# A hybrid decoder layer: GLA values and output gates by seven products of halves, placed among another branch's units

## The chip, the cores and the metric

The kernel runs on one core of one Trainium2 chip. The metric is the device time of one execution in microseconds (us). On the core, TensorE (PE) multiplies matrices, VectorE (DVE) and ScalarE (ACT) do elementwise work, GpSimd (POOL) and SyncE (SP) issue transfers. Each engine runs its own list of instructions in order and waits for the others by semaphores; a matmul writes to one of eight PSUM banks, and a bank is reused only when its reader has read it.

## The reference

One layer on 512 tokens of width 1024, all in float32. Cut to what matters:

```python
h = rms_norm(x, norm_mix)
z_rnn, z_q, z_k, z_v, z_g, z_dec, z_mq, z_gate = split(h @ w_in)       # v, g: 768 wide, dec: 16
out_a = rg_lru(causal_dwconv(z_rnn))                                   # branch 0, a linear recurrence
alpha = log_sigmoid(z_dec @ w_decay + b) / 16
o = rms_norm_per_head(chunked_gla(z_q, z_k, z_v, alpha))               # branch 1, 4 heads: dk 96, dv 192
out_b = o * silu(z_g)
out_c = cross_attention(z_mq, mem)                                     # branch 2
merged = sum over branches of sigmoid(z_gate[n]) * (out[n] @ w_branch[n])
x = x + merged @ w_out
x = x + (gelu(gate) * val) @ w_down,   gate, val = causal_dwconv(rms_norm(x) @ w_up)
return rms_norm(x)
```

In chunked_gla, q is scaled by exp(g), k by exp(-g) and by exp(g_last - g), where g is the running sum of alpha in a chunk.

## The kernel before

A float32 product is made of three products at a faster matmul type: each operand is split into a high and a low half (`split`: ACT copies the high half, DVE subtracts it to get the low one), and `mm3` adds high x high, high x low and low x high in one PSUM bank. So a product of 512 tokens with 1024 inputs and n outputs takes 4 token tiles x 8 slices x 3 = 96 matmuls with n moving columns.

The program is a list of **units** and **steps**. A unit is a weight tile with the product that uses it: SP loads the tile ('raw', three buffers), ACT and DVE split it into 'whi' and 'wlo' (three buffers each), and this is issued two units ahead (`AHEAD`). Steps are other work; `weave(units, steps)` spreads steps evenly behind units. A scheduler at build time orders each engine's instructions out of this list. Intermediates live in slots of 512 columns: `fslot` for float32 (named f in the profile), `rslot` for split halves (r), `mslot` (m). Five PSUM banks (mm) serve the large products, three (sm) the small ones.

For each of the three branches and eight column blocks d, `branch(n, acts, d)` gives two units: the gate (24 matmuls of 512 columns from hh and hl, the halves of h; ACT takes its sigmoid, L541, which frees the bank) and the projection of the branch's output (18 matmuls of 512 columns; DVE multiplies it by the gate, L547 or L549, and adds it, L550). The order is branch 2, then 0, then 1. Around the change the program runs:
- branch 2's sixteen units (b2), woven with the recurrence of branch 0: squares, scans (L630), gates, and the split of its output into r tiles by `split`;
- `v_units(0)`: the first half of v with the decay inputs beside it (400 columns), 96 matmuls, copied out by ACT (L682);
- branch 0's sixteen units (b0), woven with the decay steps: `decay_in`, four `decay_logit`, `decay_log`, four `decay_apply` (exponentials on ACT, the products with q and k on DVE, L748 to L753);
- v_units(1) and g_units(0) (384 columns), woven with `k_end` (transposes of the scaled k, L760), `intra` (scores) and `state`;
- g_units(1) and eight held gates for branch 1 (`hold`), woven with `gla_out` (the output of one token tile and two heads, and its norm, per tile) and `gla_flip` (the transpose back to channels);
- branch 1's projections, w_out, and the second half of the layer.

In that second half `down_fast` already does a product of w_down by seven products of halves in place of eight: operands are quartered, sums of quarters are multiplied, and the results are combined. The sums of weight quarters are made by DMAs that add into the tile in SBUF (`accum_op`, on POOL's queue).

Of the kernel before, what the change touches and what calls it, by code (L numbers as in the profile page):

```python
# [8 lines left out]
F32 = mybir.dt.float32  # L9
# [9 lines left out]
P = 128  # L19
# [21 lines left out]
NRAW = 3  # L41
# [14 lines left out]
def trunk(ctx: ExitStack, tc: tile.TileContext, x, xT, mem, memT, par, wdecay, wch, wvd, wvg, wmk,  # L56
# [221 lines left out]

    hh = hpool.tile([P, KD, S], F32R, name="hh", tag="hh")
# [182 lines left out]

    def piece(ps, i):
# [179 lines left out]

    each = lambda fn, bs: [lambda b=b: fn(b) for b in bs]
# [10 lines left out]
    weave(b2[12:], each(lru_square, hi) + [lambda: lru_root(1)] + each(lru_scan, hi))  # L655
# [52 lines left out]
    ea, gc = [], []  # L708

# [83 lines left out]
    def gla_out(t, hp):  # L793
        ps = sbank((P, 2, DV))
        for j in range(2):
            h = 2 * hp + j
            nc.tensor.matmul(ps[:, j, :], lhsT=sT[h][:, t, :], rhs=vt[t][hp][:, j, :], start=True, stop=t == 0)  # L797
            if t:
                nc.tensor.matmul(ps[:, j, :], lhsT=qi[h][:, t * P:(t + 1) * P], rhs=states[hp][t][:, j, :],  # L799
                                 start=False, stop=True)  # L800
        o = fslot((P, 2, DV))
        nc.vector.tensor_copy(o, ps)
        ss, tot = stat(2), stat(2)
        for j in range(2):
            meansq(o[:, j, :], ss[:, j:j + 1], DV)
        nc.vector.tensor_scalar(out=tot, in0=ss, scalar1=EPS, scalar2=None, op0=ALU.add)
        y = rsqrt(tot)
        for j in range(2):
            g = sg[t][hp][:, j, :]
            nc.vector.scalar_tensor_tensor(out=g, in0=o[:, j, :], scalar=y[:, j:j + 1], in1=g,  # L810
                                           op0=ALU.mult, op1=ALU.mult)
# [46 lines left out]
    def gain_rows(src):  # L858
        gb[0] = hpool.tile([P, D], F32, name=nm("gain"), tag="gain")
        with tc.issue_after(loads[-1].ins):  # L860
            nc.sync.dma_start(gb[0], src)
# [98 lines left out]

    HT = S // 2
    kept = {}

    def down_fast(at, np, acts, first, last):


        raw, w, a_in, a_sp, banks = {}, {}, {}, {}, {}

        def src(q, p):
            return wdown[at + p, int(q[1]) - 1, int(q[2]) - 1]

        def load(q, p):
            raw[q, p] = [fslot() for _ in range(2)]
            for j in range(2):
                loads.append(nc.sync.dma_start(raw[q, p][j], src(q, p)[:, j, :]))  # L980

        def add(to, q, p):

            for j in range(2):
                nc.gpsimd.dma_start(raw[to, p][j], src(q, p)[:, j, :], accum_op=ALU.add)  # L985

        def ready(key, q, p):
            hi = wpool.tile([P, 2, S], F32R, tag="whi", name=nm("whi"))
            lo = wpool.tile([P, 2, S], F32R, tag="wlo", name=nm("wlo"))
            if q in ("B21", "B22"):  # L990
                t = wpool.tile([P, 2, S], F32, tag="raw", name=nm("raw"), bufs=NRAW)
                loads.append(nc.sync.dma_start(t, src(q, p)))
                split(hi, lo, t)
            else:
                for j in range(2):
                    split(hi[:, j, :], lo[:, j, :], raw[q, p][j])
            w[key, p] = hi, lo
# [54 lines left out]
        def run(key, p):  # L1052
            (hi, lo), ws = a_sp.pop((key, p)), w.pop((key, p))
            b = key[0]
            for i in range(2):
                if key[1] == "1" and p == 0:
                    banks[b, i] = bank()
                tk = slice(i * P, (i + 1) * P)
                mm3(banks[b, i], [(hi[:, j, tk], lo[:, j, tk], ws[0][:, j, :], ws[1][:, j, :]) for j in range(2)],
                    key[1] == "1" and p == 0, p == np - 1, key[1] != "1")  # L1060
                if p == np - 1:
                    read(key, i, banks[b, i])

        pre = {
            "a1": ("B11", [(6, lambda p: load("B11", p)), (3, sums)]),
            "a2": ("B21", []),
            "c1": ("B11", [(6, lambda p: add("B11", "B12", p))]),
            "c2": ("B22", [(3, sum4)]),
            "b1": ("B11", [(6, lambda p: add("B11", "B22", p))]),
            "b2": ("B12", [(10, lambda p: load("B12", p)), (7, lambda p: add("B12", "B22", p))]),  # L1070
            "b3": ("B11", [(6, lambda p: add("B11", "B21", p))]),
        }
        us = []
        for key, (q, before) in pre.items():
            for p in range(np):
                us.append(([(n, lambda f=f, p=p: f(p)) for n, f in before] +
                           [(AHEAD, lambda key=key, q=q, p=p: ready(key, q, p)),
                            (1 if key == "a1" else 2, lambda key=key, p=p: act_ready(key, p))],
                           lambda key=key, p=p: run(key, p)))
        return us  # L1080

    def final_left(t):

        b = stat(1)
        nc.vector.tensor_scalar(out=b, in0=msq[t][:, 0:1], scalar1=EPS, scalar2=None, op0=ALU.add)
        xg = fslot()
        nc.gpsimd.tensor_tensor(out=xg, in0=x2[t][0], in1=gb[0][:, :HB], op=ALU.mult)
        lefts[t] = b, xg
# [3 lines left out]
    def final(t):  # L1092
# [6 lines left out]
        nc.vector.tensor_tensor(out=xr, in0=x2[t][1], in1=gb[0][:, HB:], op=ALU.mult)  # L1099
# [18 lines left out]
    for fast, up in ((down_fast(0, 3, acts[0], True, False), up_units(range(12, 20), acts[1].append)),  # L1118
                     (down_fast(3, 2, acts[1], False, True), up_units(range(20, NF), halves))):
        for i, u in enumerate(up):  # L1120
            unit(*u)
            for f in fast[len(fast) * i // len(up):len(fast) * (i + 1) // len(up)]:
                made_unit(*f)
# [7 lines left out]
def _layouts(np, v):  # L1131
# [45 lines left out]
    for j in range(3):  # L1177
# [9 lines left out]
        "wch": wch, "wvd": tok(np.concatenate([vv[:, :384], dec], axis=1), 400),  # L1187
        "wvg": np.concatenate([tok(vv[:, 384:], 384), tok(gg, 384)]),
# [26 lines left out]
```

## Time and profile before

| what | value |
|---|---|
| median of 3 runs | 940.05 us (939.97 to 940.52) |
| profiled execution, own time | 940.39 us |
| its span (first to last instruction) | 938.7 us |
| granted TensorE clock, mean | 0.998 |
| busy: PE, DVE, ACT, POOL | 927.6, 612.0, 483.1, 47.4 us |
| end of branch 2's last product | 258.09 us from the span's start |
| v_units(0) | 258.09 to 275.58 us |
| transfers | 106.46 MB, 113 GB/s on average |

In the rows below the columns of a timeline are: start, duration, engine, source line, operation, output <- inputs by name, shape, count, and in brackets the idle time before with its releaser. Durations of matmuls overlap, so the time of one is read from the starts of neighbours.

### The profile page before, as it was taken

To read this page: it belongs to the slowest core of one execution; us is meant where nothing else is said; L and a number is where in the kernel's file an instruction comes from. 1 tells how busy PE (TensorE), PEld (TensorE's weight loads), DVE (VectorE), ACT (ScalarE), POOL (GpSimd) and SP (SyncE) were. 2 spreads that over 40 slices of the span, in tenths; PEclk is the share of its full clock that TensorE was granted. 3 is DMA by queue.
4 is the path that set the end of the run, shared out by engine and by line. 5 is a ranking of instruction groups with operands and counts; after the bars stand their busy time and mean duration, and the time that the engine had idled before them with its cause. 6 is when DMAs were issued, how large, how long until landed. Compare 5 with 4: busy or idle time off the path is not lost.

```text
span 938.7 us, 11903 instructions
## 1 busy us (share of the span) xinstructions
PE 927.6 (99%) x4462; PEld 787.4 (84%) x4462; DVE 612.0 (65%) x1113; ACT 483.1 (51%) x767; POOL 47.4 (5%) x67
## 2 busy tenths in 40 slices
PE   8999999999999999999999999999999999999996
PEld 7899888888897789998888898888888888888885
DVE  7897745565754584475566665555686676598765
ACT  7655545685875765333334424344355444445544
POOL 0000000000000000000000000000010130012102
PEclk9999999999999999999999999999999999999999
DMA  6445212223232223222246401333463685357712
GB/s 230 159 126 189 90 56 72 73 68 99 75 111 96 68 84 102 73 91 84 68 139 224 159 23 45 97 106 112 136 118 134 151 222 124 105 133 180 181 45 90
DMA packets 38043, 106.46 MB, mean 113 GB/s; under 512 B 4369, under 2 KB 5537, under 8 KB 37985
## 3 DMA queue, kind: packets, MB, share of 16 engines
q1 hardware_dynamic: 31648, 94.16, 30.9%
q0 software_dynamic: 5760, 10.49, 6.9%
q10 hardware_dynamic: 576, 1.05, 0.3%
q8 instruction: 35, 0.57, 0.3%
q14 instruction: 24, 0.19, 0.1%
HBM read 103.58 MB, written 2.10 MB: 113 GB/s over the span
## 4 chain that ended last, share of the span: by engine, by line
PE 95%; DVE 3%; ACT 1%; DMA 1%; issue 0%; SPq 0%; ACTq 0%; DVEq 0%
PE mm L102 88%; PE sm L102 3%; PE mm L338 1%; DVE wlo L96 1%; PE sm L797 1%; DMA m<-in_xT 1%; DVE r L96 0%; PE sm L799 0%; PE sm L783 0%; DVE m L306 0%; PE sm L770 0%; PE sm L905 0%; PE sm L818 0%; DVE hl L96 0%; PE sm L512 0%
## 5 line engine op out<-in xcount | busy, mean ns | idle before, releaser
L96 DVE TENSOR_TENSOR wlo<-raw,whi 128x1024 fp32r<-128x1024 f32 (+3 forms) x163 | 179.4, 1104 | 173.8 <-ACT whi L95 79.8
L95 ACT ACTIVATE whi<-raw 128x1024 fp32r<-128x1024 f32 (+3 forms) x163 | 156.5, 964 | 201.1 <-PE mm L102 173.2
L102 PE MATMUL mm<-h2l,whi 128*128 128x512 f32 x360 | 140.1, 389 | 0.0
L102 PE MATMUL mm<-h2h,whi 128*128 128x512 f32 x360 | 139.9, 389 | 0.0
L102 PE MATMUL mm<-whi,r 128*128 128x512 f32 (+1 forms) x440 | 136.8, 381 | 0.0
L102 PE MATMUL mm<-hh,whi 128*128 128x512 f32 x288 | 113.9, 396 | 0.0
L102 PE MATMUL mm<-hl,whi 128*128 128x512 f32 x288 | 112.6, 391 | 0.0
L102 PE MATMUL mm<-r,whi 128*128 128x512 f32 (+1 forms) x448 | 98.3, 368 | 0.0
L102 PEld LDWEIGHTS mm<-whi,r 128*128 128x128 f32 x440 | 82.2, 188 | 14.8
L102 PEld LDWEIGHTS mm<-r,whi 128*128 128x128 f32 x448 | 77.9, 189 | 14.6 <-issue 0.8
L102 PE MATMUL mm<-h2h,wlo 128*128 128x512 f32 x360 | 88.9, 389 | 0.0
L102 PE MATMUL mm<-wlo,r 128*128 128x512 f32 (+1 forms) x220 | 84.0, 382 | 0.2 <-DVE wlo L96 0.2
L102 PEld LDWEIGHTS mm<-h2l,whi 128*128 128x128 f32 x360 | 67.6, 188 | 14.0
L102 PEld LDWEIGHTS mm<-h2h,wlo 128*128 128x128 f32 x360 | 67.6, 188 | 14.1
L102 PEld LDWEIGHTS mm<-h2h,whi 128*128 128x128 f32 x360 | 67.5, 188 | 13.9
L922 DVE SCALAR_TENSOR_TENSOR f<-mm,prm,f 128x511 f32<-128x511 f32 x96 | 71.4, 745 | 6.9 <-ACT f L920 6.1
L102 PE MATMUL mm<-hh,wlo 128*128 128x512 f32 x288 | 71.2, 389 | 0.0
L102 PEld LDWEIGHTS mm<-hh,whi 128*128 128x128 f32 x288 | 54.2, 188 | 11.6 <-issue 0.4
L102 PEld LDWEIGHTS mm<-hh,wlo 128*128 128x128 f32 x288 | 54.1, 188 | 11.2
L102 PEld LDWEIGHTS mm<-hl,whi 128*128 128x128 f32 x288 | 54.1, 188 | 10.7
L985 POOL DMA_DIRECT2D f<-in_wdown x40 | 35.1, 997 | 495.7 <-DMA f<-in_wdown 333.3
L920 ACT ACTIVATE f<-mm,prm 128x512 f32<-128x512 f32 x48 | 37.5, 780 | 35.8 <-PE mm L102 35.8
(212 smaller groups left out, 1340.7 us busy)
## 6 DMA issues: line engine op xcount, KB each, us to landing
raw<-in_wup SPq DMA_DIRECT2D x48, 512.0 KB, 3.5
raw<-in_wch SPq DMA_DIRECT2D x40, 512.0 KB, 3.3
f<-in_wdown POOLq DMA_DIRECT2D x40, 256.0 KB, 5.3
raw<-in_wbr SPq DMA_DIRECT2D x24, 384.0 KB, 3.0
raw<-in_wdown SPq DMA_DIRECT2D x14, 512.0 KB, 3.9
f<-in_wdown SPq DMA_DIRECT2D x20, 256.0 KB, 4.4
raw<-in_wvg SPq DMA_DIRECT2D x12, 384.0 KB, 3.0
raw<-in_wout SPq DMA_DIRECT2D x8, 512.0 KB, 3.6
```

The source lines that it names most:

```text
L95: nc.scalar.activation(hi, src, AF.Copy)
L96: (eng or nc.vector).tensor_tensor(out=lo, in0=src, in1=hi.bitcast(F32), op=ALU.subtract)
L102: nc.tensor.matmul(ps, lhsT=l, rhs=r, start=first and i == 0, stop=last and i == len(seq) - 1, skip_group_check=more)
L338: nc.tensor.matmul(ps[u], lhsT=a, rhs=b, start=q == 0 and i in (0, 2), stop=q == KD - 2 and i >= len(seq) - 2)
L797: nc.tensor.matmul(ps[:, j, :], lhsT=sT[h][:, t, :], rhs=vt[t][hp][:, j, :], start=True, stop=t == 0)
L920: nc.scalar.activation(a, ps, AF.Identity, scale=col(C_FCW + 96 + f), bias=col(C_FCB + f))
L922: nc.vector.scalar_tensor_tensor(out=a[:, j:], in0=ps[:, :S - j], scalar=col(C_FCW + 48 * (2 - j) + f), in1=a[:, j:], op0=ALU.mult, op1=AL ...
L985: nc.gpsimd.dma_start(raw[to, p][j], src(q, p)[:, j, :], accum_op=ALU.add)
```

## The change

**Seven products.** The units of v (with the decay inputs, padded to 2 x 400 columns) and of g are replaced by `seven`, a general form of `down_fast`'s code: h is quartered into token halves and input halves, the weights into input halves and output halves. The seven products are called a1, a2, c1, c2, b1, b2, b3; each has two units (p = 0, 1) of 12 matmuls, of 400 columns for v and 384 for g. a1 and a2 share two banks, c1 and c2 two, and so on: a product whose name ends in 2 or 3 adds onto the bank after the first has been read. B11 is loaded into slots six units ahead; B12, B22 and B21 are added to it in place, by POOL's queue.

**Sums of h.** c1, c2, b1 and b2 need sums of quarters of h. `h_sums` makes them in two steps woven in at the end of branch 2's last four units: four adds hh + hl, four combinations and four splits for each p, 24 instructions on DVE and 8 on ACT.

**Order.** `blend` puts the 28 new units behind the first seven units of branch 0, four behind each. The decay steps go over the rest of branch 0 and two held gates (eleven units); the other GLA steps follow held gates two to seven.

**q and k** are written to DRAM by POOL when they are made, and read back by `qk_back` at the start of the decay steps. **The norm** of the GLA outputs is taken for four token tiles at once (`gla_norm`). There are four raw buffers in place of three, and the gain rows lie in two slots.

```diff
+    def seven(src, n, np, lhs, pre, read, far=AHEAD):
...
+        def add(to, q, p):
+            for j in range(2):
+                nc.gpsimd.dma_start(raw[to, p][j], src(q, p)[:, j, :], accum_op=ALU.add)
...
+        def run(key, p):
+            ws = w.pop((key, p))
+            b = key[0]
+            for i in range(2):
+                if key[1] == "1" and p == 0:
+                    banks[b, i] = bank((P, n))
+                mm3(banks[b, i], [(*lhs(key, p, j, i), ws[0][:, j, :], ws[1][:, j, :]) for j in range(2)],
+                    key[1] == "1" and p == 0, p == np - 1, key[1] != "1")
+                if p == np - 1:
+                    read(key, i, banks[b, i])
+        steps = {
+            "a1": ("B11", [(6, lambda p: load("B11", p))]),
+            "a2": ("B21", [(far, lambda p: direct("B21", p))]),
+            "c1": ("B11", [(6, lambda p: add("B11", "B12", p))]),
+            "c2": ("B22", [(far, lambda p: direct("B22", p))]),
+            "b1": ("B11", [(6, lambda p: add("B11", "B22", p))]),
+            "b2": ("B12", [(10, lambda p: load("B12", p)), (7, lambda p: add("B12", "B22", p))]),
+            "b3": ("B11", [(6, lambda p: add("B11", "B21", p))]),
+        }
...
+    def blend(us, fast, steps=()):
+        for i, u in enumerate(us):
+            unit(*u)
+            for l, f in ((fast, lambda v: made_unit(*v)), (steps, step)):
+                for v in l[len(l) * i // len(us):len(l) * (i + 1) // len(us)]:
+                    f(v)
...
     def qk_evac(ps, i):
         f = fslot()
         nc.scalar.activation(f[:DK], ps[:DK], AF.Copy, scale=DK ** -0.5 if i < 4 else 1.0)
-        (qs if i < 4 else ks).append(f)
+        nc.gpsimd.dma_start(qk[i], f[:DK])
...
+    def h_sums(p):
+        tt = nc.vector.tensor_tensor
+        f = {}
+        for r, c in ((2, 1), (2, 2), (1, 1), (1, 2)):
+            f[r, c] = fslot((P, 2, HT))
+            a, b = (v[:, 4 * c - 4 + 2 * p:4 * c - 2 + 2 * p, (r - 1) * HT:r * HT].bitcast(F32) for v in (hh, hl))
+            tt(out=f[r, c], in0=a, in1=b, op=ALU.add)
+        tt(out=f[2, 2], in0=f[2, 1], in1=f[2, 2], op=ALU.subtract)
+        tt(out=f[2, 1], in0=f[1, 1], in1=f[2, 1], op=ALU.subtract)
+        tt(out=f[1, 1], in0=f[2, 2], in1=f[1, 1], op=ALU.subtract)
+        tt(out=f[1, 2], in0=f[1, 2], in1=f[1, 1], op=ALU.add)
+        for key, a in (("c1", f[2, 2]), ("c2", f[1, 2]), ("b1", f[1, 1]), ("b2", f[2, 1])):
+            hsum[key, p] = rslot((P, 2, HT)), rslot((P, 2, HT))
+            split(*hsum[key, p], a)
...
-    weave(b2[12:], each(lru_square, hi) + [lambda: lru_root(1)] + each(lru_scan, hi))
+    weave(b2[12:], each(lru_square, hi) + [lambda: lru_root(1)] + each(lru_scan, hi) + each(h_sums, range(2)))
...
+    def v_read(key, i, ps):
+        if key == "a1":
+            gla["k", i] = fslot((P, HP + LOW))
+            nc.scalar.activation(gla["k", i], ps, AF.Copy)
...
+        elif key in ("c1", "c2"):
+            tt(out=flat2(vt[t][1]), in0=z, in1=gla["k", i][:, :HP], op=ALU.subtract)
...
-    weave(v_units(0), [])
     step(causal)
     b0 = [u for d in range(KD) for u in branch(0, oa, d)]
-    weave(b0, [decay_in] + [lambda h=h: decay_logit(h) for h in range(H)] + [decay_log] +
-          [lambda h=h: decay_apply(h) for h in range(H)])
-    weave(v_units(1) + g_units(0), [lambda t=t: k_end(t) for t in range(NT)] + [lambda h=h: intra(h) for h in range(H)] +
-          [lambda n=n, hp=hp: state(n, hp) for hp in range(2) for n in range(NT - 1)])
...
-    weave(g_units(1) + [hold(d) for d in range(KD)],
-          [lambda t=t: gla_out(t, 0) for t in range(NT)] + [lambda m=m: gla_flip(m) for m in range(3)] +
-          [lambda t=t: gla_out(t, 1) for t in range(NT)] + [lambda m=m: gla_flip(m) for m in range(3, 6)])
+    held = [hold(d) for d in range(KD)]
+    blend(b0[:7], v_fast() + g_fast())
+    weave(b0[7:] + held[:2], [decay_in, qk_back] + [lambda h=h: decay_logit(h) for h in range(H)] + [decay_log] +
+          [lambda h=h: decay_apply(h) for h in range(H)])
+    tiles = range(NT)
+    for u, steps in zip(held[2:], (
+            each(k_end, tiles) + each(intra, range(H)),
+            [lambda n=n, hp=hp: state(n, hp) for n in range(2) for hp in range(2)],
+            [lambda hp=hp: state(2, hp) for hp in range(2)] + [lambda t=t: gla_out(t, 0) for t in tiles],
+            [lambda: gla_norm(0)] + [lambda t=t: gla_out(t, 1) for t in tiles],
+            each(gla_flip, range(3)) + [lambda: gla_norm(1)],
+            each(gla_flip, range(3, 6)))):
+        weave([u], steps)
```

The next rows are those of ACT behind the last split of the recurrence's output, before (r_2499 is that split; f_26xx are the first copies of v out of their banks, f_2675 is the first gate of branch 0):

```order
L95 ACTIVATE r_2499<-f_2491 128x512
L95 ACTIVATE whi_2599<-raw_2597 128x768
L682 ACTIVATE f_2609<-mm_2509 128x384
L682 ACTIVATE f_2619<-mm_2510 128x384
L682 ACTIVATE f_2628<-mm_2511 128x384
L682 ACTIVATE f_2637<-mm_2512 128x384
L95 ACTIVATE whi_2646<-raw_2644 128x1024
L95 ACTIVATE whi_2679<-raw_2677 128x768
L541 ACTIVATE f_2675<-mm_2650 128x512
```

And the same place now, behind the recurrence's last split and the high weights of branch 0's first projection, whi_2671 (whi_2691 is the weight of c1, r_2547 to r_2583 are splits of the sums of h, f_2626 is the first gate, whose bank the second group of c1, mm_2767, takes next; mm_2634 and mm_2641 are a1):

```order
L96 ACTIVATE whi_2691<-f_2286 128x400
L96 ACTIVATE whi_2691<-f_2287 128x400
L96 ACTIVATE r_2547<-f_2537 128x512
L96 ACTIVATE r_2551<-f_2535 128x512
L96 ACTIVATE r_2555<-f_2531 128x512
L96 ACTIVATE r_2571<-f_2561 128x512
L96 ACTIVATE r_2575<-f_2565 128x512
L96 ACTIVATE r_2579<-f_2563 128x512
L96 ACTIVATE r_2583<-f_2559 128x512
L619 ACTIVATE f_2626<-mm_2601 128x512
L790 ACTIVATE f_2659<-mm_2634 128x400
L790 ACTIVATE f_2667<-mm_2641 128x400
```

The four copies of v are gone from here, and eight splits of sums (r_2543 stands just above these rows) and two of a weight's halves stand ahead of the first gate's sigmoid.

DVE at that place now (r_2528 is the low half of the recurrence's last output; L732 are the adds hh + hl, L733 to L736 the combinations, L97 the low halves):

```order
L97 TENSOR_TENSOR r_2528<-f_2490,r_2527 128x512
L732 TENSOR_TENSOR f_2531<-hh,hl 128x512
L732 TENSOR_TENSOR f_2533<-hh,hl 128x512
L732 TENSOR_TENSOR f_2535<-hh,hl 128x512
L732 TENSOR_TENSOR f_2537<-hh,hl 128x512
L733 TENSOR_TENSOR f_2533<-f_2531,f_2533 128x512
L97 TENSOR_TENSOR wlo_2672<-raw_2669,whi_2671 128x768
L734 TENSOR_TENSOR f_2531<-f_2535,f_2531 128x512
L97 TENSOR_TENSOR r_2544<-f_2533,r_2543 128x512
L735 TENSOR_TENSOR f_2535<-f_2533,f_2535 128x512
L97 TENSOR_TENSOR wlo_2692<-f_2286,whi_2691 128x400
L736 TENSOR_TENSOR f_2537<-f_2537,f_2535 128x512
```

Before, the low half of the recurrence's last output was followed on DVE by one weight split and four copies of 16 columns; now all the sums of h stand behind it, with the low weights of the first projection (wlo_2672) among them.

DVE at the end of the decays now (L885 to L901 are the steps of `decay_apply`; f_3685, scaled by L896, is the last head's k that the transposes of `k_end` read):

```order
L890 TENSOR_TENSOR f_3851<-f_3643 96x512
L97 TENSOR_TENSOR wlo_3867<-raw_3864,whi_3866 128x1024
L885 TENSOR_TENSOR f_3685<-f_3685,f_3684 96x512
L897 COPY dec<-f_3853 96x4
L887 SCALAR_TENSOR_TENSOR f_3684<-chm,f_3685 96x512
L896 TENSOR_TENSOR f_3644<-f_3644,f_3532 96x512
L898 TENSOR_TENSOR f_3853<-f_3853,f_3524 96x512
L888 TENSOR_TENSOR f_3685<-f_3684 96x512
L900 TENSOR_TENSOR f_3524<-f_3524,f_3852 96x512
L901 TENSOR_TENSOR f_3532<-f_3532,f_3851 96x512
L97 TENSOR_TENSOR wlo_3916<-raw_3913,whi_3915 128x1024
L896 TENSOR_TENSOR f_3685<-f_3685,f_3534 96x512
```

The steps of all four heads now run beside seven units, four of which are gates whose 1024-wide weights DVE also splits, and `k_end` follows the third of the held gates.

More of the change, by code (lines that the diff above doesn't have):

```diff
@@ L274, in token_held, with load, direct, ready @@
         return [(dram[i], 2 * n, lambda w, i=i: fn(i, w), 2) for i in range(nk)]
+    def seven(src, n, np, lhs, pre, read, far=AHEAD):
+        raw, w, banks = {}, {}, {}
+        def load(q, p):
+            raw[q, p] = [fslot((P, n)) for _ in range(2)]
+            for j in range(2):
+                loads.append(nc.sync.dma_start(raw[q, p][j], src(q, p)[:, j, :]))
+        def add(to, q, p):
+            for j in range(2):
+                nc.gpsimd.dma_start(raw[to, p][j], src(q, p)[:, j, :], accum_op=ALU.add)
+        def direct(q, p):
+            raw[q, p] = wpool.tile([P, 2, n], F32, tag="raw", name=nm("raw"), bufs=NRAW)
+            loads.append(nc.sync.dma_start(raw[q, p], src(q, p)))
+        def ready(key, q, p):
+            hi = wpool.tile([P, 2, n], F32R, tag="whi", name=nm("whi"))
+            lo = wpool.tile([P, 2, n], F32R, tag="wlo", name=nm("wlo"))
+            if isinstance(raw[q, p], list):
+                for j in range(2):
+                    split(hi[:, j, :], lo[:, j, :], raw[q, p][j])
+            else:
+                split(hi, lo, raw.pop((q, p)))
+            w[key, p] = hi, lo
+        def run(key, p):
[17 more added lines that the diff above has]
+        }
+        us = []
+        for key, (q, before) in steps.items():
+            for p in range(np):
+                us.append(([(m, lambda f=f, p=p: f(p)) for m, f in before] +
+                           [(AHEAD, lambda key=key, q=q, p=p: ready(key, q, p))] +
+                           [(m, lambda f=f, p=p: f(p)) for m, f in pre.get(key, ())],
+                           lambda key=key, p=p: run(key, p)))
+        return us
@@ L461, in trunk @@
     qs, ks, zr = [], [], []
+    dpool = pool("spill", 1, space=bass.MemoryType.DRAM)
+    qk = [dpool.tile([DK, S], F32, tag=f"qk{i}", name=nm("qk")) for i in range(2 * H)]
     def piece(ps, i):
@@ L642, in lru_scan, with h_lhs @@
                 oa.append(rr)
+    hsum = {}
+    def h_sums(p):
[12 more added lines that the diff above has]
+            split(*hsum[key, p], a)
+    def h_lhs(key, p, j, i):
+        tk = slice(i * P, (i + 1) * P)
+        if (key, p) in hsum:
+            return tuple(a[:, j, tk] for a in hsum[key, p])
+        k = 2 * p + j + (4 if key in ("a2", "b3") else 0)
+        t = 2 + i if key == "b3" else i
+        return hh[:, k, t * P:(t + 1) * P], hl[:, k, t * P:(t + 1) * P]
     each = lambda fn, bs: [lambda b=b: fn(b) for b in bs]
@@ new lines, in silu, with g_read @@
+    def silu(t, hp, z):
+        s = fslot((P, 2, DV))
+        nc.scalar.activation(flat2(s), z, AF.Sigmoid)
+        nc.vector.tensor_tensor(out=flat2(s), in0=flat2(s), in1=z, op=ALU.mult)
+        sg[t][hp] = s
+    def g_read(key, i, z):
+        tt = nc.vector.tensor_tensor
+        if key == "a1":
+            gla["g", i] = fslot((P, HP))
+            nc.scalar.activation(gla["g", i], z, AF.Copy)
+        elif key == "a2":
+            silu(i, 0, z)
+        elif key in ("c1", "c2"):
+            d = gla["g", key, i] = fslot((P, HP))
+            tt(out=d, in0=z, in1=gla["g", i], op=ALU.subtract)
+        elif key in ("b1", "b2"):
+            d = gla.pop(("g", "c2" if key == "b1" else "c1", i))
+            tt(out=d, in0=d, in1=z, op=ALU.subtract)
+            silu(i if key == "b1" else i + 2, 1, d)
+        else:
+            d = gla.pop(("g", i))
+            tt(out=d, in0=d, in1=z, op=ALU.add)
+            silu(i + 2, 0, d)
@@ L697, in decay_in, with v_fast, g_fast @@
+    def v_fast():
+        return seven(lambda q, p: wv[p, int(q[1]) - 1, int(q[2]) - 1], HP + LOW, 2, h_lhs, {}, v_read, 4)
+    def g_fast():
+        return seven(lambda q, p: wg[p, int(q[1]) - 1, int(q[2]) - 1], HP, 2, h_lhs, {}, g_read, 4)
     def decay_in():
@@ L708, in trunk, with qk_back @@
     ea, gc = [], []
+    def qk_back():
+        for i in range(2 * H):
+            f = fslot()
+            nc.gpsimd.dma_start(f[:DK], qk[i])
+            (qs if i < 4 else ks).append(f)
     def decay_logit(h):
@@ L802, in gla_out, with gla_norm @@
         nc.vector.tensor_copy(o, ps)
-        ss, tot = stat(2), stat(2)
+        if t == 0:
+            gla["ss", hp] = stat(2 * NT)
         for j in range(2):
-            meansq(o[:, j, :], ss[:, j:j + 1], DV)
-        nc.vector.tensor_scalar(out=tot, in0=ss, scalar1=EPS, scalar2=None, op0=ALU.add)
-        y = rsqrt(tot)
[L808 to L811, printed above, removed]
+            meansq(o[:, j, :], gla["ss", hp][:, 2 * t + j:2 * t + j + 1], DV)
+        gla["o", t, hp] = o
+    def gla_norm(hp):
+        tot = stat(2 * NT)
+        nc.vector.tensor_scalar(out=tot, in0=gla["ss", hp], scalar1=EPS, scalar2=None, op0=ALU.add)
+        y = rsqrt(tot)
+        for t in range(NT):
+            o = gla.pop(("o", t, hp))
+            for j in range(2):
+                g = sg[t][hp][:, j, :]
+                nc.vector.scalar_tensor_tensor(out=g, in0=o[:, j, :], scalar=y[:, 2 * t + j:2 * t + j + 1], in1=g,
+                                               op0=ALU.mult, op1=ALU.mult)
     ob = []
@@ L858, in gain_rows @@
     def gain_rows(src):
-        gb[0] = hpool.tile([P, D], F32, name=nm("gain"), tag="gain")
-        with tc.issue_after(loads[-1].ins):
-            nc.sync.dma_start(gb[0], src)
+        for j in range(2):
+            gb[j] = fslot()
+            with tc.issue_after(loads[-1].ins):
+                nc.sync.dma_start(gb[j], src[:, j * HB:(j + 1) * HB])
     msq = {}
@@ L956, in up_units @@
         return us
-    HT = S // 2
     kept = {}
     def down_fast(at, np, acts, first, last):
[L972 to L997, printed above, removed]
+        a_in, a_sp = {}, {}
         def sums(p):
@@ L1050, in read @@
                       "b2": (2 + i, 1, ps, ALU.subtract), "b3": (2 + i, 0, ps)}[key])
[L1052 to L1080, printed above, removed]
+        pre = {k: [(2, lambda p, k=k: act_ready(k, p))] for k in ("a2", "c1", "b1", "b2", "b3")}
+        pre["a1"] = [(3, sums), (1, lambda p: act_ready("a1", p))]
+        pre["c2"] = [(3, sum4), (2, lambda p: act_ready("c2", p))]
+        return seven(lambda q, p: wdown[at + p, int(q[1]) - 1, int(q[2]) - 1], HB, np,
+                     lambda key, p, j, i: tuple(a[:, j, i * P:(i + 1) * P] for a in a_sp[key, p]), pre, read)
     def final_left(t):
@@ L1086, in final_left @@
         xg = fslot()
[L1087 removed]
+        nc.gpsimd.tensor_tensor(out=xg, in0=x2[t][0], in1=gb[0], op=ALU.mult)
         lefts[t] = b, xg
@@ L1117, in trunk @@
     weave(up_units(range(12), acts[0].append, 3), [])
[L1118 to L1123, printed above, removed]
+    blend(up_units(range(12, 20), acts[1].append), down_fast(0, 3, acts[0], True, False))
+    blend(up_units(range(20, NF), halves), down_fast(3, 2, acts[1], False, True))
     step(lambda: gain_rows(gfin))
```

50 lines of the change are left out of this document (27 added, 23 removed).

## The prediction

> **What bounds the kernel now.** I read the page's totals first, then its chain of waits.
>
> ```profile
> span 938.7 us, 11903 instructions
> PE 927.6 (99%) x4462; PEld 787.4 (84%) x4462; DVE 612.0 (65%) x1113; ACT 483.1 (51%) x767; POOL 47.4 (5%) x67
> PE 95%; DVE 3%; ACT 1%; DMA 1%; issue 0%; SPq 0%; ACTq 0%; DVEq 0%
> ```
>
> TensorE is the bound: a matmul removed is time gained, and a wait at which it runs dry is time lost one for one. What a matmul costs is the pitch between starts, so I read the timeline of PE at the three widths:
>
> ```profile
> 258.09 0.34 PE L102 MATMUL mm<-whi,hh 128*128 128x400 f32 x1
> 275.58 0.39 PE L102 MATMUL mm<-hh,whi 128*128 128x512 f32 x1
> 306.83 0.39 PE L102 MATMUL mm<-hh,whi 128*128 128x512 f32 x1
> 310.23 0.39 PE L102 MATMUL mm<-hl,whi 128*128 128x512 f32 x1
> 387.84 0.47 PE L102 MATMUL mm<-whi,hh 128*128 128x384 f32 x1
> 388.15 0.34 PE L102 MATMUL mm<-wlo,hh 128*128 128x384 f32 x1
> 391.80 0.51 PE L102 MATMUL mm<-whi,hl 128*128 128x384 f32 x2
> ```
>
> The 96 matmuls of the first value half start between 258.09 and 275.58: 0.182 us each. At 512 wide 15 steps take 3.40 us, 0.227 each; at 384 wide 21 steps take 3.65 us, 0.174 each. The step 387.84 to 388.15, into another group of banks, is 0.31: such a change costs 0.1 to 0.13 more.
>
> Last, the stretches by engine, to see who has room where the change puts work:
>
> ```profile
> 250.00:275.00 25.00, 25.00 (x130) 23.60 (x129) 19.84 (x27) 21.64 (x33) 2.23 (x2) 1.00 0.38 113
> 325.00:350.00 25.00, 25.00 (x112) 20.71 (x111) 22.49 (x34) 18.57 (x24) 1.58 (x3) 1.00 0.27 85
> 750.00:775.00 25.00, 25.00 (x112) 20.71 (x111) 17.28 (x25) 12.02 (x19) 8.78 (x10) 1.00 0.86 223
> ```
>
> The columns are PE, PEld, DVE, ACT, POOL, clock, DMA share. At 250 to 275, the end of branch 2, ACT is busy 21.6 of 25 us and DVE 19.8: they finish the recurrence. At 325 to 350, the decays, DVE is busy 22.5. Elsewhere there is room. TensorE idles nowhere, but the change puts work into just these two places.
>
> **Part 1: the products.** Values cost 96 x 0.182 + 96 x 0.174 = 34.2 us; seven products of 2 x 12 matmuls, all 400 wide, are 168 x 0.182 = 30.6: -3.6. Gates cost 192 x 0.174 = 33.4; 168 x 0.174 = 29.2: -4.2. Together **-7.8**. GLA's small products (scores, states, outputs) are now gathered behind six units; by the order PE goes 25 times from them to another group before and 16 times after: 9 x 0.1 = **-0.9**, between 0 and -1.2.
>
> **Part 2: the start of the blend.** Before, the end of branch 2 was followed by the four value units, which need only hh, hl and weights. ACT and DVE used them to end the recurrence:
>
> ```profile
> 255.84 1.28 ACT L638 ACTIVATE f<-f 32x512 f32<-32x512 f32 x2
> 261.71 2.56 ACT L638 ACTIVATE f<-f 32x512 f32<-32x512 f32 x4
> 264.30 0.87 ACT L95 ACTIVATE whi<-raw 128x800 fp32r<-128x800 f32 x1
> 269.26 0.62 ACT L95 ACTIVATE r<-f 128x512 fp32r<-128x512 f32 x1
> 270.53 0.68 DVE L96 TENSOR_TENSOR r<-f,r 128x512 fp32r<-128x512 f32 x1
> 281.04 2.88 PE L102 MATMUL mm<-r,whi 128*128 128x512 f32 x12
> ```
>
> The last half of the recurrence's output was ready at 271.2, its first product began at 281.04: ten us of slack, made by 17.5 us of value units and 5.4 of the gate. Now that product follows the gate and a1 alone, and 24 DVE rows and 8 ACT rows of h_sums are queued behind the recurrence.
>
> I set zero at the end of branch 2 (258.09). Without waits PE would reach: the gate's end, 24 x 0.227 = 5.4; a1's end, 24 x 0.182 more, 9.8; the projection's end (18 matmuls), 13.9; six matmuls of c1, 15.0; then c1's other bank, mm_2767. That bank is the one the gate's result lay in, and the sigmoid L619 that frees it stands on ACT behind all eight h_sums splits (the second list of order above). DVE prices:
>
> ```profile
> 341.57 0.68 DVE L752 TENSOR_TENSOR f<-f,f 96x512 f32<-96x512 f32 x1
> 342.17 0.68 DVE L550 TENSOR_TENSOR m<-m,f 128x512 f32<-128x512 f32 x1
> 336.32 0.95 DVE L96 TENSOR_TENSOR wlo<-raw,whi 128x768 fp32r<-128x768 f32 x1
> 337.19 0.68 DVE L742 TENSOR_TENSOR f<-f 96x512 f32<-96x512 f32 x1
> ```
>
> A row of 512 is 0.60 us by pitch (0.68 as shown), one of 768 is 0.87; 400 wide I take as 0.48 by width. Then:
> - ACT's recurrence rows are those of before, one for one, with an 800-wide weight split in place of a 1024-wide one; they end at +11.6, and the projection's high weights whi_2671 at +12.6. PE has waited 2.8.
> - DVE takes r_2528 until +12.4, five h_sums adds (3.0), the low weights wlo_2672 (0.87): +16.3. The projection ends at 17.7.
> - 18 more DVE rows up to the sum f_2565 for ACT's r_2575 and those after it: 16 x 0.60 + 2 x 0.48 = 10.6, with 0.4 for handovers: +27.3.
> - ACT: r_2575, r_2579, r_2583 at 0.64 (the 512-wide r row above with its gap), 1.9; the sigmoid 0.60: +29.8.
>
> mm_2767 starts at 29.8 in place of 15.0: **+14.8**. Bounds: if DVE kept up at no cost, ACT alone would set it, 12.6 + 8 x 0.64 + 2 x 0.5 + 0.6 = 19.4, +4.4; if both ran strictly by turns, 12.4 + 14.4 (the DVE rows) + 6.7 (the ACT rows) = 33.5 and a few handovers, +19.5. I take the value near the upper end because the sums are a chain: each split waits for its DVE sum.
>
> **Part 3: the clock.** The wait before mm_2767 is one idle piece of 9 to 10 us. The end of the kernel shows what TensorE's clock does then (column 1.00, 0.76, 0.50; the last matmul ends near 930.6):
>
> ```profile
> 931.00:933.00 2.00, 0.00 (x0) 0.00 (x0) 1.95 (x11) 1.23 (x4) 0.00 (x0) 1.00 0.22 82
> 933.00:935.00 2.00, 0.00 (x0) 0.00 (x0) 0.95 (x4) 1.24 (x2) 0.00 (x0) 0.76 0.46 169
> 935.00:937.00 2.00, 0.00 (x0) 0.00 (x0) 0.00 (x0) 0.00 (x0) 0.00 (x0) 0.50 0.96 355
> 1.12 4.21 PE L209 MATMUL sm<-warm 128*128 128x128 f32 x18 [1.12 <-DVE warm L205]
> 285.13 0.60 PE L702 MATMUL sm<-ident,f 128*16 128x128 f32 x4
> 285.48 0.48 PE L102 MATMUL mm<-hh,whi 128*128 128x512 f32 x1
> ```
>
> 0.76 over two us is full speed to 934.0 and half after, 3.4 us past the last matmul. How long it stays low after work resumes no row shows. If as long as it took to fall, 3.4 us at half rate, it costs **+1.7**. Bounds: 0, and the start of the kernel, where 18 small matmuls take 234 ns each against 88 (four in 285.13 to 285.48), 18 x 0.146 = 2.6.
>
> On this the Trainium skill ("TensorE: Matmul & The Clock Gate", section on the HAM clock gate) says that the gate halves the clock after an idle window of about 3.4 us and opens it after about 3.4 us of sustained work. The fall agrees with the 3.4 us above; the return no run here shows yet. By that rule the loss is the same 1.7; were the rule not to hold within a kernel, the sum would be 1.7 less.
>
> **Part 4: inside the blend.** c2 adds onto c1's bank after DVE's L798 has read it, and that row stands behind two weight splits (0.9 each): I count **+0.7**, bounds 0 and 2.
>
> **Part 5: the decays.** From the last logit to the first k_end transposes PE had:
>
> ```profile
> 317.55 0.94 PE L102 MATMUL sm<-r,r 16*96 16x512 f32 x3
> 360.82 0.49 PE L760 MATMUL sm<-ident,f 96*128 96x96 f32 x4
> 323.05 2.33 DVE L739 TENSOR_TENSOR_SCAN f<-chm,f 96x512 f32<-96x512 f32 x2
> 332.00 1.21 DVE L96 TENSOR_TENSOR wlo<-raw,whi 128x1024 fp32r<-128x1024 f32 x1
> 333.13 0.68 DVE L550 TENSOR_TENSOR m<-m,f 128x512 f32<-128x512 f32 x1
> ```
>
> 42 us of cover. Now it is 132 matmuls (two projections of 18, four gates of 24) x 0.227 = 30.0 and eight transposes that need only heads 0 to 2 (0.7): 30.7. DVE, from the end of that stretch's first projection (18 x 0.227 = 4.1), has 29 rows x 0.60, five 1024-wide splits x 1.13, four scans x 1.165, three copies x 0.2 = 28.3, up to f_3685 (the last list of order above): 32.4. **+1.7**, bounds 0 and 6: before, DVE idled some 4.5 us in that stretch for ACT's exponentials and table loads, and those waits would add.
>
> **Costed at nothing.** q and k through DRAM: eight small POOL writes that nobody waits for; read back after the last accumulation, and first needed some 35 us later, against
>
> ```profile
> f<-in_wdown POOLq DMA_DIRECT2D x40, 256.0 KB, 5.3
> L985 POOL DMA_DIRECT2D f<-in_wdown x40 | 35.1, 997 | 495.7 <-DMA f<-in_wdown 333.3
> ```
>
> 8 x 1.0 + 5.3 = 13.3; without that cover, up to 13.3. The accumulating transfers of B11 and B12: each has the four units between a weight's split and its next one, 11 us, against two issues and a landing, 2.0 + 5.3 = 7.3; the window 750 to 775 shows the same scheme at a DMA share of 0.86 and PE full. The norm of four tiles adds a wait for the fourth, a chain of a dozen rows (7.6), under at least 12 us of held gates; uncovered, 7.6. Gain rows in two pieces: the same bytes, as early.
>
> **Sum**, on the profiled execution's own 940.39: -7.8 - 0.9 + 14.8 + 1.7 + 0.7 + 1.7 = +10.2, 950.6; the median of the runs lies 0.34 lower: **950**. All low bounds give 936, all high ones 962.
>
> **Rivals.**
> - *The sums are hidden.* The 14.8 at the start falls to ACT's 4.4, no clock loss, no wait at the decays: 940.05 - 7.8 - 0.9 + 4.4 + 0.7 = **936.5**, faster. For it: most of h_sums needs nothing of the recurrence. Against it: the rows stand behind the recurrence on an in-order DVE, at 0.60 each. It decides wherever the start costs under about 6 us, since then the losses no longer outweigh 8.7.
> - *Loss and gain cancel*, with a start near 7 and no clock loss: 939 to 941. It needs a narrow coincidence.
> - *The accumulations come late.* At twice the landing (10.6 + 2.0 = 12.6 against 11) each of the eight later accumulated unit pairs waits 1.6, 13 us, of which the start's wait hides about a third: **958**. For it: DVE and ACT run late at the start, and a slot is accumulated into only after its split. Against it: the same scheme further down.
>
> **Chances.** Forecast 0.68, with its own range 945 to 955; hidden 0.14; cancel 0.06; late 0.12. A difference under 0.2% is about what a measurement of this kernel cannot tell from none: 938.2 to 941.9 is "same". Faster 0.15, same 0.06, slower 0.79. The range, 940 to 958, leaves out the hidden case and the far end of the late one.
>
> **What would show it.** PE's busy total lower by about 8, with pitches 0.182 and 0.174 in the new products. An idle piece of PE of 9 to 10 us before a 400-wide matmul, some 20 us after branch 2's end, released by ACT's L619, with a clock below 1 behind it; before it a shorter one at the projection, released by the weight split; the DVE rows L732 to L736 running all after branch 2's end. A short idle before the L908 transposes, released by DVE L896. The forecast is wrong if PE runs through the blend's start, or if its waits there name accumulated weights (DMA).

## The result: 1.5% slower, and where the time went

The changed kernel takes 954.04 us (median of 4 runs, 953.96 to 954.67), the kernel before 940.17 beside it: a ratio of 1.0149, with a 95% interval of 1.0131 to 1.0166. The forecast was 950, in a range of 940 to 958. The profiled execution took 953.96, that of before 940.39: 13.6 us more.

The totals and the chain of the changed kernel:

```profile
span 952.3 us, 12010 instructions
PE 925.5 (97%) x4414; PEld 781.4 (82%) x4414; DVE 637.6 (67%) x1111; ACT 500.4 (53%) x806; POOL 82.9 (9%) x115
PE 87%; ACT 5%; DVE 5%; issue 1%; DMA 0%; SPq 0%; ACTq 0%; DVEq 0%
```

TensorE does 48 matmuls fewer, 24 each for v and g, and is busy 97% of the span in place of 99: it now waits. The table of what PE waited for (engine, line, releaser: us in total, times, longest) names the places:

```profile
PE mm L103 <- ACT f L619: 9.6, 1, 9.6
PE mm L103 <- ACT whi L96: 2.8, 1, 2.8
PE sm L908 <- DVE f L896: 1.5, 1, 1.5
PE mm L103 <- DVE wlo L97: 1.2, 3, 0.5
PE sm L210 <- DVE warm L206: 1.1, 1, 1.1
PE mm L413 <- ACT r L361: 0.9, 1, 0.9
PE mm L103 <- DVE f L798: 0.5, 1, 0.5
```

The waits at L210 and L413 are those of the kernel's start, which the kernel before has too. Four of the others (L619, whi, L896, L798) were forecast, with the releasers that were forecast. The waits for low weights (wlo) were not; two of the three, 1.0 us, lie ahead of the long wait and are hidden by what it waits for. None names a DMA. The timeline of PE at the start of the blend, which begins where branch 2 ends, at 258.16 (24 matmuls of a gate, 5.44 us, before the first a1 matmul at 263.60):

```profile
270.92 4.38 PE L103 MATMUL mm<-r,whi 128*128 128x512 f32 x12 [2.79 <-ACT whi L96]
277.77 0.45 PE L103 MATMUL mm<-wlo,r 128*128 128x400 f32 x1 [0.54 <-DVE wlo L97]
278.86 0.45 PE L103 MATMUL mm<-wlo,r 128*128 128x400 f32 x1 [0.46 <-DVE wlo L97]
289.32 0.70 PE L103 MATMUL mm<-whi,r 128*128 128x400 f32 x1 [9.64 <-ACT f L619]
292.82 0.34 PE L103 MATMUL mm<-wlo,hh 128*128 128x400 f32 x1
299.55 0.42 PE L103 MATMUL mm<-whi,r 128*128 128x400 f32 x1 [0.53 <-DVE f L798]
303.98 0.40 PE L103 MATMUL mm<-hh,whi 128*128 128x512 f32 x1
```

c1's second group starts at 289.32, 31.2 us after branch 2's end, where 15.0 would have done. Once nothing waits, 24 products of 400 columns go from 299.55 to 303.98, 0.185 each with a change of group in it: the price of the products is as before.

What DVE and ACT did in that time (DVE's timeline first, then ACT's):

```profile
270.56 0.68 DVE L97 TENSOR_TENSOR r<-f,r 128x512 fp32r<-128x512 f32 x1
271.16 2.49 DVE L732 TENSOR_TENSOR f<-hh,hl 128x512 f32<-128x512 f32 x4
274.17 0.95 DVE L97 TENSOR_TENSOR wlo<-raw,whi 128x768 fp32r<-128x768 f32 x1
280.83 2.93 DVE L732 TENSOR_TENSOR f<-hh,hl 128x512 f32<-128x512 f32 x4
286.39 0.69 DVE L736 TENSOR_TENSOR f<-f,f 128x512 f32<-128x512 f32 x1
```

```profile
284.40 0.63 ACT L96 ACTIVATE r<-f 128x512 fp32r<-128x512 f32 x1 [4.37 <-DVE f L733]
287.11 1.67 ACT L96 ACTIVATE r<-f 128x512 fp32r<-128x512 f32 x3 [2.09 <-DVE f L736]
288.69 0.58 ACT L619 ACTIVATE f<-mm 128x512 f32<-128x512 f32 x1
```

DVE closes the recurrence (270.56), then makes the sums of h until 287, with no pause longer than 0.22 us and with the splits of some weights between them; ACT waits for it row by row. The gate that L619 reads had been in its bank since 263.8. Its sigmoid takes 0.58 us, and it was run 25 us later, behind the recurrence's tail and all the sums.

### The profile page after: what moved, and what is told of

It is laid out like the page before. It is cut to its first block, busy times and chain, and to the rows that moved or that the text cites. A ratio compares the mean times of both kernels' runs of the same rounds, so it can differ in the third digit from the quotient of the medians.

```text
span 952.3 us, 12010 instructions
## 1 busy us (share of the span) xinstructions
PE 925.5 (97%) x4414; PEld 781.4 (82%) x4414; DVE 637.6 (67%) x1111; ACT 500.4 (53%) x806; POOL 82.9 (9%) x115
## 4 chain that ended last, share of the span: by engine, by line
PE 87%; ACT 5%; DVE 5%; issue 1%; DMA 0%; SPq 0%; ACTq 0%; DVEq 0%
PE mm L103 81%; PE sm L103 3%; DVE wlo L97 1%; ACT f L716 1%; PE mm L413 1%; DVE r L97 1%; ACT whi L96 1%; ACT r L96 1%; PE sm L945 1%; DMA m<-in_xT 0%; PE sm L931 0%; PE sm L947 0%; ACT L619 0%; DVE m L381 0%; PE sm L918 0%
## 5 line engine op out<-in xcount | busy, mean ns | idle before, releaser
L97 DVE TENSOR_TENSOR wlo<-raw,whi 128x1024 fp32r<-128x1024 f32 (+2 forms) x155 | 172.0, 1114 | 158.0 <-ACT whi L96 72.4
L96 ACT ACTIVATE whi<-raw 128x1024 fp32r<-128x1024 f32 (+2 forms) x155 | 149.9, 970 | 159.5 <-PE mm L103 143.8
L103 PE MATMUL mm<-whi,r 128*128 128x512 f32 (+2 forms) x568 | 171.6, 373 | 10.3 <-ACT f L619 9.6
L103 PEld LDWEIGHTS mm<-whi,r 128*128 128x128 f32 x568 | 105.7, 188 | 26.1 <-ACT f L619 10.0
L103 PE MATMUL mm<-wlo,r 128*128 128x512 f32 (+2 forms) x284 | 106.0, 373 | 1.2 <-DVE wlo L97 1.2
L96 ACT ACTIVATE whi<-f 128x512 fp32r<-128x512 f32 (+2 forms) x90 | 48.1, 579 | 75.4 <-PE mm L103 69.1
L97 DVE TENSOR_TENSOR wlo<-f,whi 128x512 fp32r<-128x512 f32 (+2 forms) x90 | 53.7, 632 | 42.9 <-ACT whi L96 23.2
```

Of the source, the lines that this page charges most:

```text
L96: nc.scalar.activation(hi, src, AF.Copy)
L97: (eng or nc.vector).tensor_tensor(out=lo, in0=src, in1=hi.bitcast(F32), op=ALU.subtract)
L103: nc.tensor.matmul(ps, lhsT=l, rhs=r, start=first and i == 0, stop=last and i == len(seq) - 1, skip_group_check=more)
```

## The experiments

The theory is that of the prediction: the long wait is a matter of the place in two queues, where the sums of h stand ahead of the reader of a bank that PE needs. Rivals: too little TensorE work between the recurrence and its first product; late accumulating transfers; too much work for DVE and ACT in this stretch wherever it stands.

**e1: without the sums.**

```diff
-    weave(b2[12:], ... + each(lru_scan, hi) + each(h_sums, range(2)))
+    weave(b2[12:], ... + each(lru_scan, hi))
```

> The changed kernel without h_sums: c1, c2, b1 and b2 take a quarter of h itself in place of a sum of quarters (so these four products are of other numbers; the count and shape of the matmuls stay). Theory (the sums stand ahead of the gate's sigmoid on ACT and DVE): the 9.6 us wait, the two waits of 0.5 for low weights, the 0.5 wait before c2 and the half clock behind the long wait (1.6) go; the 2.8 us wait at the first projection stays, since the recurrence's tail is the same. 954.0 - 9.6 - 1.0 - 0.5 - 1.6 = about 941. Rival, too little cover between the recurrence and its first product whatever stands in the queues: above 950. Rival, late accumulating transfers: unchanged, 954.

Measured: 940.2 us (938.33 to 941.79, 10 runs), 0.9998 of the kernel before (0.9988 to 1.0008). Of PE's waits:

```profile
PE mm L103 <- ACT whi L96: 2.8, 1, 2.8
PE sm L908 <- DVE f L896: 1.5, 1, 1.5
PE mm L103 <- DVE wlo L97: 0.2, 1, 0.2
```

The waits of 9.6, 1.0 and 0.5 are gone with the sums; the 2.8 at the projection and the 1.5 before k_end stay. The transfers were the same in number and size, and the added weights of v landed even later (6.6 us in the median against 5.1), so the DMA rival falls, and so does that of the cover, as the recurrence's tail alone costs 2.8.

**e2: a1 and a2 of v and g first.**

```diff
-    blend(b0[:7], v_fast() + g_fast())
+    vf, gf = v_fast(), g_fast()
+    blend(b0[:7], vf[:4] + gf[:4] + vf[4:] + gf[4:])
```

> The changed kernel with the 28 new units in another order: a1 and a2 of v, a1 and a2 of g, then the rest, four behind each of the same seven units. h_sums stays where it is. TensorE has four more units (8.4 us) to do before the first product that needs a sum of h. Theory (it is the place in ACT's and DVE's queues, not the distance in matmuls): a bank still waits for a reader behind the sums, so the long wait of 9 to 12 us stays and the time is 952 to 957. Rival (the sums come too late for c1, and more distance would cover them): 954.0 - 8.4 - 1.6 = about 944.

Measured: 954.1 us (953.54 to 955.02), 1.0148 (1.0133 to 1.0163).

```profile
PE mm L103 <- ACT f L790: 11.8, 1, 11.8
PE mm L103 <- ACT whi L96: 2.8, 1, 2.8
```

With four more units ahead of the first use of a sum the wait is not shorter, it is 11.8, and it stands before a2, which uses no sum. Another reader stands at its end now, the copy of a1 (L790), whose bank a2 needs, and it too is behind the sums on ACT. Distance in matmuls does not help when the banks come free through the queue that is late.

**e5: the sums behind the first new units.** The order of e2, and:

```diff
-    weave(b2[12:], ... + each(lru_scan, hi) + each(h_sums, range(2)))
+    weave(b2[12:], ... + each(lru_scan, hi))
...
+            made_unit(*v)
+            if i == 0 and j in (1, 3):
+                step(lambda j=j: h_sums(j // 2))
```

> The order of e2 (a1 and a2 of v and g first), and h_sums moved in the program from the end of branch 2 to behind the second and the fourth of the new units. The same work on DVE and ACT, later in their queues. Theory (the place in the queue, ahead of the readers of banks, makes the long wait): the wait of 9 to 12 us goes, what DVE and ACT are short of is spread over several short waits of 4 to 5 us in all, and the 2.8 at the projection stays: 954.1 - 11.8 - 2 (clock) + 4.5 = about 945. Rival (DVE and ACT have no room for these sums in this stretch, wherever they stand): 952 or more.

Measured: 947.22 us (943.2 to 948.07), 1.0065 (1.0047 to 1.0083).

```profile
PE mm L103 <- ACT whi L96: 3.3, 2, 2.8
PE mm L103 <- DVE wlo L97: 3.2, 2, 3.0
```

The same 24 DVE and 8 ACT instructions, later in the queues, cost some 4 us of waits in place of 12, and the time falls by 7 against e2, to 2 above the expectation. Part of the third rival stands: they are still not free, as a 3.0 wait for a weight's low half shows. The waits are those of the execution of 943.2, at a mean granted clock of 0.998; the other three took 946.9 to 948.1 at 0.992, and no trace of them is kept.

**e6: the sums by POOL, in branch 2.** As e5, with the adds and combinations apart from the splits:

```diff
     def h_sums(p):
-        tt = nc.vector.tensor_tensor
+        tt = nc.gpsimd.tensor_tensor
...
-    weave(b2[8:12], [...])
+    weave(b2[8:12], each(h_sums, range(2)) + [...])
...
+            if i == 0 and j in (1, 3):
+                step(lambda j=j: h_split(j // 2))
```

> As e5, but the adds and combinations of h_sums (16 of the 24 DVE instructions) are made by POOL, some 40 us earlier, within branch 2; only the splits remain behind the new units. Theory: like the kernel without sums, 940.2, within 1.5: the 2.8 at the projection, the 1.5 before k_end and no wait of more than 1 us for the sums. Rival (POOL's elementwise work, 1.3 us an instruction, or the splits alone keep the sums late): 944 or more.

Measured: 942.57 us (940.87 to 943.54, 7 runs), 1.0024 (1.0013 to 1.0036): short of the expectation by 0.9. At the blend's start there is the 2.8 of e1, and none for a sum. What is new in the waits, beside 0.4 before c2, lies in branch 2, where POOL works beside DVE. First one of POOL's rows of this kernel, then groups of DVE (line, operation, shape, count | busy, mean ns | idle) between 198 and 226 us, of e1 and of e6:

```profile
201.84 1.74 POOL L733 TENSOR_TENSOR f<-f,f 128x512 f32<-128x512 f32 x1
```

```profile
L688 DVE TENSOR_TENSOR f<-f 96x512 f32<-96x512 f32 x4 | 2.7, 682 | 1.4 <-ACT f L680 1.4
L625 DVE TENSOR_TENSOR m<-mm,f 128x512 f32<-128x512 f32 x3 | 2.1, 689 | 2.2 <-PE mm L103 2.2
```

```profile
L688 DVE TENSOR_TENSOR f<-f 96x512 f32<-96x512 f32 x4 | 6.4, 1618 | 0.6 <-ACT f L680 0.6
L625 DVE TENSOR_TENSOR m<-mm,f 128x512 f32<-128x512 f32 x2 | 1.4, 676 | 0.0
```

While POOL adds, a DVE instruction with both operands in SBUF takes 1618 ns in place of 682; one with an operand in PSUM (L625) takes 676 as ever. The Trainium skill ("SBUF — State Buffer", section "Who interferes with whom") says that a DVE instruction with two SBUF inputs contends with a GpSimd instruction that reads SBUF; these rows agree. The delay passed on to PE is two short waits (0.57 at 215.18 and 0.20 at 219.30). They are the smaller part of the 4.0 us between the profiled executions of e6 and e1 (942.34 and 938.33): behind the same 2.8 us wait the clock stayed up in e1, and here it was 0.59 and 0.55 from 272 to 276, which is 1.7 us lost.

**e7: and the decays earlier.** As e6, with the decay's input and logits behind the last five new units, and each of the seven units of branch 0 behind two of its four new ones in place of ahead of them:

```diff
+            if j == 2:
+                unit(*u)
...
+            if i == 5 and j == 3:
+                step(decay_in)
+            if i == 6:
+                step(lambda j=j: decay_logit(j))
...
-    weave(b0[7:] + held[:2], [decay_in, qk_back] + [lambda h=h: decay_logit(h) for h in range(H)] + [decay_log] + ...)
+    weave(b0[7:] + held[:2], [qk_back, decay_log] + ...)
```

> As e6, and the decay's input and its four logits are woven behind the last five of the new units in place of the first units after them, so the decay's products on DVE end earlier; the first gate stands behind two of the new units. Theory: the wait of 1.5 before k_end goes too, 940.2 - 1.7 and up to 1 more = 937.5 to 938.5, faster than the kernel before (940.2). Rival (the decays then stand in the way of the gates' combinations, and waits of the same size come up there): 940 or more.

Measured: 938.63 us (937.73 to 939.41, 11 runs), 0.9980 (0.9971 to 0.9989) of the kernel before: 0.1 above the expectation, and faster than both kernels, than the one before by 0.2%, with no run in common (939.77 to 940.95 beside it). The wait before k_end is gone, and no other came in its place; what is left at the blend's start is the wait for weights that ACT splits behind the recurrence's tail (1.9; the other wait in this row is the 0.57 of branch 2):

```profile
PE mm L103 <- ACT whi L96: 2.5, 2, 1.9
```

Two things were moved at once here, and no run divides the gain on e6 between them.

**e3 and e8: useless work in the waits.** 40 and 58 products of 128 columns (each is two matmuls in the profile), behind the first four new units:

```diff
+    def fill():
+        ps = sbank((P, P))
+        for _ in range(NFILL):
+            nc.tensor.matmul(ps, lhsT=warm, rhs=warm, start=True, stop=True)
```

> The changed kernel with 40 useless small products (128x128, some 9 us of TensorE work) issued behind the first four new units, ahead of the first projection. The waits there add up to 13.4 us, and they end when ACT and DVE are done, so the added work fits into them. Theory (the half clock behind the waits costs 3.3 us on top of them): the clock stays up and the time falls by 1.6 to 3.3, to 950.7 to 952.4. Rival (the clock costs nothing, the slower matmuls only fill waits): 954.0, or a little more.

Measured with 40: 954.67 us (953.83 to 955.16), no gain, where 950.7 to 952.4 was expected. The timeline of PE:

```profile
268.20 9.09 PE L753 MATMUL sm<-warm 128*128 128x128 f32 x80
284.01 0.45 PE L104 MATMUL mm<-wlo,r 128*128 128x400 f32 x1 [2.43 <-DVE wlo L98]
286.30 0.70 PE L104 MATMUL mm<-wlo,r 128*128 128x400 f32 x1 [1.65 <-DVE wlo L98]
289.08 0.70 PE L104 MATMUL mm<-whi,r 128*128 128x400 f32 x1 [1.42 <-ACT f L620]
289.92 0.54 PE L104 MATMUL mm<-whi,r 128*128 128x400 f32 x1
290.25 0.54 PE L104 MATMUL mm<-whi,hh 128*128 128x400 f32 x1
```

Nine us of added TensorE work did not put off the end of the wait: 289.08 against 289.32. That is the plainest sign that PE was not the bound there. But the work came too early; from 281.6 on there were three waits with a few matmuls between, and the clock fell all the same (0.33 us between 289.92 and 290.25, in place of 0.18).

> As e3 with 58 useless products in place of 40, about 12.9 us, nearly all of the 13.4 us of waits at the start of the blend. In e3 7.7 us of mostly idle time were left behind the fill, and the clock fell as before. Theory: with at most 3 us left the clock stays up, and what the slow matmuls cost (ten in 3.5 us where they take 1.8) is saved: 954.0 - 1.6 = 952.4. Rival (the clock costs nothing): 954 to 955.

Measured with 58: 952.54 us (951.68 to 953.57, 4 runs), ratio 1.0130 (1.0117 to 1.0144).

```profile
268.07 13.11 PE L753 MATMUL sm<-warm 128*128 128x128 f32 x116
288.00 0.45 PE L104 MATMUL mm<-wlo,r 128*128 128x400 f32 x1 [0.75 <-DVE wlo L98]
289.37 0.35 PE L104 MATMUL mm<-wlo,hh 128*128 128x400 f32 x1
289.55 0.35 PE L104 MATMUL mm<-whi,hh 128*128 128x400 f32 x1
```

Now the step is 0.18 (289.37 to 289.55), and with 13 us of useless products the kernel takes 1.5 us less. The runs of the two kernels do not overlap (951.68 to 953.57 against 953.96 to 954.67), but the intervals of their ratios do, so it is the steps between the rows that carry the verdict. Not all of the gain is the clock's: of the 2.0 us between the profiled executions (953.96 and 951.96), 0.7 is that c1's second group starts earlier, at 288.65 in place of 289.32, and 1.3 lies behind it.

**e4: two parts alone on the kernel before**, q and k through DRAM, and the norm of four tiles at once:

```diff
-        (qs if i < 4 else ks).append(f)
+        nc.gpsimd.dma_start(qk[i], f[:DK])
...
-    weave(b0, [decay_in] + ...)
+    weave(b0, [decay_in, qk_back] + ...)
...
+    [lambda: gla_norm(0)]      # behind the fourth tile's gla_out, ahead of the flips; gla_norm(1) likewise
```

> The kernel before with two parts of the change alone: q and k through DRAM, read back at the start of the decay steps, and the norm of four token tiles at once. Theory: both are free, 940.1 within 0.9. Rival: the read-back or the wait for the fourth tile shows, 942 or more.

Measured: 940.23 us (940.06 to 940.55, 10 runs), a ratio of 1.000 (0.999 to 1.0009). Both are free, as costed, on the kernel before.

## Why the prediction was right, point by point

| term | forecast | measured |
|---|---|---|
| products of v and g | -7.8 | -7.8 (168 + 168 matmuls at the same pitches) |
| changes to small products, short waits | -0.9 | +1.1 (what the other rows leave of 13.6) |
| start of the blend, up to mm_2767 | +14.8 | +16.2 (289.32 - 258.16 - 15.0) |
| before c2 | +0.7 | +0.7 (0.53 of wait, and the restart) |
| half clock behind the long wait | +1.7 | +1.7 (ten matmuls in 3.50 us, 289.32 to 292.82, for 1.82) |
| before k_end | +1.7 | +1.7 (1.53 of wait, and the restart) |
| sum | +10.2 | +13.6 |

**The bound and the mechanism** held. The time is slower because the sums stand ahead of L619; e1 takes the sums away and the 9.6 us wait goes, e2 and e3 show that neither distance nor TensorE's own work matters there, e5 that place does. The waits at the projection (2.8 forecast and measured) and before k_end were found by the same reckoning of rows. They are also why e1 is hardly faster than the kernel before: 940.39 - 7.8 + 2.8 + 1.7 + 1.1 is 938.2, and its profiled execution took 938.33.

**The start was mis-sized by 1.4.** r_2528 ended at +13.1 (271.24) and not +12.4. The 18 DVE rows behind the low weights took 12.0 us (275.04 to 287.08) where 10.6 and 0.4 of handovers were counted: four adds took 2.93 in place of 2.49, with POOL's mask step (L777) and its transfers beside them, and the rest are pauses of 0.1 to 0.2 at which DVE and ACT hand over. That POOL's step made the adds longer is not shown by a run. The three ACT rows and the sigmoid took 0.3 less than counted.

**The -0.9 was wrong in kind.** "A change into another group of banks costs 0.1 to 0.13 more" read one half of the step. Rows of the state products, eight ahead of a large product (before) and eight ahead of other small ones (after), show the other half:

```profile
386.68 1.46 PE L783 MATMUL sm<-f,f 128*96 128x192 f32 x8
```

```profile
455.22 1.46 PE L931 MATMUL sm<-f,f 128*96 128x192 f32 x8
456.52 0.49 PE L945 MATMUL sm<-f,f 128*128 128x192 f32 x2
```

Eight take 1.30 us up to another small one (455.22 to 456.52), but 1.16 up to the large one at 387.84 that the prediction quotes. The last small product of a group is short by the 0.14 by which the first large one behind it is long: the change costs nothing, and gathering the small products saved nothing. Of the 1.1 us on the other side, 0.3 is a step behind a transpose of the decay's input (367.14) and 0.3 one inside a product of v (within the three matmuls from 313.47); the rest is spread too thin to name.

**PE's busy total** was said to fall by 8 and fell by 2.1 (927.6 to 925.5). Slow matmuls count as busy: at half clock those of the projection took 1.7 us more and the ten behind the long wait 1.7. That the rest is the longer first matmul after each wait and the 1.1 above would fit, but is not worked out row by row. The sign that would have shown the products is the pitch, not the total.

**The rivals.** That the sums are hidden failed by the 9.6 us wait, and that loss and gain cancel by the start, which cost 16.2 where some 7 was needed. Late accumulations: no wait of PE names a transfer, and the median landing of the added weights was 5.1 us against 5.3 for those of w_down before. Of the things costed at nothing, q and k in DRAM and the norm of four are free on the kernel before (e4), and no wait of PE here names the others.

## What to carry to other kernels

Before moving work into a stretch, read what its engines' queues hold there, and look for a short instruction that frees a bank or a buffer and would stand behind the new work: it is the queue's length ahead of that reader that TensorE waits for, not the work's share of the span. Taking away matmuls only pays where the engines that prepare their operands have room; here 7.8 us were won and 16 lost in a stretch in which DVE and ACT were already at 79% and 87%, and most of it came back by moving the same work to other places in the queues (e5, e7) and two thirds of its DVE instructions to POOL (e6).

## What was not expected of the hardware

**A short wait can halve the clock, or not.** In the changed kernel the 2.8 us wait before the projection was followed by half clock, in e1 the same wait was not. Windows of PE (busy, granted clock, DMA share, GB/s), the changed kernel and then e1:

```profile
272.00:274.00 2.00, 2.00 (x7) 0.56 0.61 233
274.00:276.00 2.00, 2.00 (x7) 0.58 0.00 0
```

```profile
272.00:274.00 2.00, 2.00 (x13) 1.00 0.98 335
274.00:276.00 2.00, 2.00 (x13) 1.00 0.94 348
```

In the changed kernel it cost nothing, as c1 was waiting anyway. The traces of e2 and e5 have the same wait (2.78 and 2.79) with a clock of 1.00 behind it in these two windows, that of e6 (2.78) has 0.59 and 0.55. Of e1's executions six took 938.3 to 940.7 us with a mean clock of 0.996 or 0.997, and four 941.4 to 941.8 with 0.993 or 0.994; that these four lost the clock at this wait is not shown, as no trace of them is kept. In e7 even a wait of 1.9 us was followed by steps of 0.33 us for 400 columns:

```profile
271.33 0.62 PE L103 MATMUL mm<-whi,hh 128*128 128x384 f32 x2 [1.93 <-ACT whi L96]
274.00 0.54 PE L103 MATMUL mm<-wlo,hh 128*128 128x400 f32 x1
274.34 0.87 PE L103 MATMUL mm<-whi,hl 128*128 128x400 f32 x2
```

The Trainium skill ("TensorE: Matmul & The Clock Gate", section "Why this matters for your kernels") advises against idle gaps of more than some 3 us; here 1.9 to 2.8 were enough in some executions. Why the same gap halves the clock in one execution and not in another stays open. The return took 3.5 us after the long wait, as estimated.

**POOL's elementwise work beside DVE** made DVE's instructions of L688, with two SBUF operands, 2.4 times as long (682 to 1618 ns, e6), while most of POOL's own took some 1.74 us for 128x512, and one 4.08. An engine that looks idle is not free room when its work makes that of a busy one longer.
